# Attention trunk on one core: q, k and v of seven head pairs in product units of 512 columns over pair borders, and attention anchors set apart from the units

## The chip, the core and the metric

The kernel runs on one core of a Trainium2 chip. Its time is the device time of one execution in microseconds (us); lower is better. The names of the engines are those of the profile: PE (TensorE matmul) and PEld (its weight loads, which overlap), DVE (VectorE), ACT (ScalarE), POOL (GpSimd), SP (SyncE, which issues nearly all loads and stores). Each engine works through its own instructions in the order of the program and waits on semaphores for the others.

## What is computed

Two residual layers over 512 tokens of 1,024 features, all in float32. Layer 0 mixes tokens by attention in three dilated windows (dilations 1, 4 and 16, radius 64, 32 and 64 steps of the dilation), layer 1 by a short gated convolution; an MLP with a squared ReLU stands behind each. The change touches the attention of layer 0:

```python
def mixer_a(h, w_qkv, q_gain, k_gain, w_o, cos, sin):
    qkv = (h @ w_qkv).reshape(B, S, A_GROUPS, 3, A_HEADS, HEAD_DIM)
    for g in range(A_GROUPS):
        q = partial_rope(rms_norm(qkv[:, :, g, 0], q_gain[g]), cos, sin)
        k = partial_rope(rms_norm(qkv[:, :, g, 1], k_gain[g]), cos, sin)
        num, den, mx = dilated_group(q, k, qkv[:, :, g, 2], dil, radius)
    wts = jnp.exp(mx - jnp.max(mx, axis=0, keepdims=True))
    o = jnp.sum(wts[..., None] * num, axis=0) / jnp.sum(wts * den, axis=0)[..., None]
    return o.reshape(B, S, D_MODEL) @ w_o
```

## The kernel before, in words

**Products.** Every large product is done three times over: each float32 operand is split into a rounded part and a rest (wh and wl for weights, hgh and hgl for activations), and the three products that matter are added up in PSUM (line 128). A weight tile of 128 rows is loaded by SP into one of four buffers (wraw), rounded by ACT (wh, line 288), and the rest is taken by POOL (wl, line 289); for the first two tiles DVE does both. There are six buffers of wh and wl each.

**Units.** The q, k and v weights of one pair of heads are nine blocks of 128 columns (three dilation groups with q, k and v each). Before the change a pair has three product units of 384 columns: group A (q0, k0, q1), group B (k1, q2, k2) and group V (v of the three groups). A unit is 8 weight tiles (k) by 4 row tiles of the tokens (r), so 8 x 4 x 3 = 96 matmuls, in blocks of two weight tiles (of one in the first unit). It fills four PSUM banks (psG, one for each r). When a bank is full, it is evacuated at once: group A and B are copied to rawA and rawB by ACT (or DVE, by the bits of vA and vB), group V is scaled and split on ACT and DVE.

**The clock of the schedule.** The program is written out by a planner with a clock of its own, which has nothing to do with the chip's: a block adds (its weight tiles) x (its row tiles) x (its columns) / 2048, so a unit of 384 columns is 6 long and one of 512 columns 8. Every other step is a task with a position on that clock; between two matmuls of a unit the planner emits the tasks that are due. So the positions set the order of the instructions on every engine, and nothing else does. The whole of q, k and v is 144 long before and after.

**Attention of a pair.** Its steps hang on two anchors, tA and tB, the ends of the pair's units A and B; the scores' anchor tS equals tB. The offsets stand in PLACES (line 60: one row for pair 0, one for pairs 1 to 6, one for pair 7). The steps, with the names that are used below:
- *normalize group A* (sqA, rsA, mulA): squares on ACT, sums by reductions on DVE (stA, line 362), twelve small DVE instructions for the reciprocal square roots (lines 365 and 151 to 157), then products and the rotation on DVE (lines 371 to 378). The same for group B (stB), with three of four rotations on POOL.
- *fills* (TA, TB, line 387): four transposes on PE into a score bank (psT, three banks), rounded by ACT (q0h and so on, line 401), rest by DVE (q0l, line 403).
- *S0* (line 443) and *S12* (line 457): scores on PE, masked and reduced on DVE (lines 447 and 460), then exponentials on ACT.
- *weights of the groups* (W1 to W4), with two swaps of rows through PE (line 433).
- *N12 and N0* (lines 502 and 504): the products of the probabilities with the weights, half on DVE, half on POOL.
- *PT* (line 516): transposes of the probabilities into psT, split by ACT and DVE (pth and ptl); *PV* (line 544): their product with v; at the end the sum into oT (line 548).

The attention of a pair lies beside the units of the pairs that follow. The part of v for dilation 1 goes through DRAM and back (move_v0).

**The start.** x comes in eight column tiles. Each is transposed on PE (line 297), scaled and split into hgh and hgl by ACT (line 300) and DVE (a copy to oT, line 301, and the rest, line 302): an x fill. Eight squares of x on ACT (line 273) give the statistics of the first normalization (x_stats: lines 279 to 282 and 151 to 157, 14 DVE instructions of 4 columns). DVE also builds the rotation tables tabA and tabB (line 251) from loaded gains.

Of the kernel before, what the change touches and what calls it, by code (L numbers as in the profile page):

```python
# [35 lines left out]
def _constants():  # L36
# [10 lines left out]
    for n, b in enumerate((0, 1, 3)):  # L47
# [27 lines left out]
def trunk_kernel(ctx, tc, x, norm1, norm2, wqkv, qgain, kgain, wo, win, conv, wout, w1, w2, c_rope, c_m0, c_m12, out):
# [251 lines left out]
    def evacV(p):
        def f(r, ps):
            if r == 0:
                need("stats", 0, 1)  # L330
                st[p]["v"] = ptile(vp, [128, 4, 3, 2, 2, 64], R32, "v")
            v = st[p]["v"][:, r].rearrange("p g h s d -> p (g h) s d")
            split(v[:, :, 0], v[:, :, 1], ps[:, 0:384].rearrange("p (a d) -> p a d", d=64), rcol[:, r:r + 1])
            mark("evV", p)
            if r == 3:
                after(0.4, move_v0)

        def move_v0():

            v0 = st[p]["v0"] = ptile(vp, [128, 4, 2, 128], R32, "v0")  # L340
            sync.dma_start(v0d[p].rearrange("r c h s d -> c r (h s d)"),
                           f32(st[p]["v"])[:, :, 0].rearrange("p r h s d -> p r (h s d)"))

            def read(j, a):
                c = (32 * j + 16 + 16 * a) % 128
                sync.dma_start(f32(v0)[64 * a:64 * a + 64, j].rearrange("p h c -> p (h c)"),
                               v0d[p][:, c:c + 16].rearrange("r c h s d -> r c (h s d)"))
                mark("v0", p)
            for j in range(4):
                for a in range(2):  # L350
                    after(1.2 + 0.35 * (2 * j + a), lambda j=j, a=a: read(j, a))
        return f
# [228 lines left out]
    def mark(name, p):  # L581
        seen[name, p] = seen.get((name, p), 0) + 1

    def need(name, p, n):
        assert p < 0 or seen.get((name, p), 0) >= n, f"{name} of pair {p}: {seen.get((name, p), 0)} of {n} issued"

    def attn_tasks(p, tA, tB, c):


        tS = tB  # L590
# [9 lines left out]
        for r in range(4):  # L600
            put(tA + c["sqA"] + 0.25 * r, "sqA", lambda r=r: norm_sq(rawA, stA, 6, r, r < c["qA"]), ("evA", p, 4))
# [36 lines left out]
        for n, (h, i) in enumerate([(h, i) for h in range(2) for i in range(4)]):  # L638
            s = tS + c["P"] + c["dP"] * n + c["gP"] * (n > 3)
            put(s, "PT", lambda h=h, i=i: PT(p, h, i), ("N12" if i > 1 else "N0", p, 8))  # L640
            put(s + c["lP"], "PV", lambda h=h, i=i, n=n: PV(p, h, i, n % 4 == 0, n % 4 == 3), ("PT", p, n + 1), ("evV", p, 4),
                ("v0", p, 8))
# [374 lines left out]
```

## Time and profile before

| | |
|---|---|
| median of 3 runs (lowest, highest) | 1487.7 us (1486.6, 1487.86) |
| the profiled execution's own time | 1487.62 us |
| its span, first to last instruction | 1485.8 us |
| mean granted clock of PE | 0.997 |
| q, k, v and attention | 6.8 to 546.7 us of the span |
| output projection of the attention | 546.7 to 603.8 us |
| MLP, convolution, second MLP | 603.8 to 1485.8 us |

Times in the views count from the start of the span. A row of a timeline has start, length, engine, line, operation, output<-inputs, shapes and count, and in brackets the idle time of the engine before it and who ended it. A matmul's row names the moving operand first, then the stationary one; its length is modelled and longer than the distance to the next, so the rate is read from the starts. "st" is a bank of psT, "g" one of psG, "sm" the scores of a pair.

### The profile page before, as it was taken

The numbers are of one execution on the slowest core, as the hardware profiler recorded it, in microseconds if no ns is written. First come the engines' busy times: TensorE is split into PE (matmuls) and PEld (weight loads), VectorE is DVE, ScalarE is ACT, GpSimd is POOL, SyncE is SP. The second block draws the span as 40 slices with busy tenths as digits, with TensorE's granted clock in tenths as the row PEclk, the third lists the DMA queues.
The fourth block names the chain that finished last, engine by engine and source line by source line (L and its number), as shares of the span: only waits on it lengthen the run. The fifth ranks groups of instructions, "written<-read, shape, count | busy, mean of one in ns | idle before, by whom it ended". The sixth has DMA issues, their size and how long they took to land.

```text
span 1485.8 us, 22525 instructions
## 1 busy us (share of the span) xinstructions
PE 1474.2 (99%) x7900; PEld 1291.2 (87%) x7900; DVE 708.0 (48%) x1460; ACT 663.2 (45%) x1359; POOL 702.9 (47%) x671
## 2 busy tenths in 40 slices
PE   9899999999999999999999999999999999999998
PEld 8899999999999998888888888878888888888887
DVE  6777667676767684822021223554447330122222
ACT  5456565656556573544342332433343443333320
POOL 4444444536454444455444445444455554544442
PEclk9999999999999999999999999999999999999999
DMA  6432322323132323232222222233332222222222
GB/s 170 132 104 69 94 87 78 102 65 115 54 115 67 101 98 130 96 113 93 95 97 99 99 97 95 82 89 93 100 113 100 99 93 92 100 99 96 99 89 85
DMA packets 164509, 144.76 MB, mean 97 GB/s; under 512 B 13812, under 2 KB 125484, under 8 KB 164396
## 3 DMA queue, kind: packets, MB, share of 16 engines
q1 hardware_dynamic: 164076, 143.06, 30.7%
q8 instruction: 62, 1.02, 0.3%
q14 instruction: 51, 0.42, 0.1%
q10 hardware_dynamic: 320, 0.27, 0.1%
HBM read 134.89 MB, written 8.39 MB: 96 GB/s over the span
## 4 chain that ended last, share of the span: by engine, by line
PE 93%; DVE 3%; issue 1%; ACT 1%; DMA 1%; SPq 1%; POOL 0%; DVEq 0%; POOLq 0%; ACTq 0%
PE g L128 85%; PE o L544 3%; PE st L516 2%; PE st L457 2%; PE st L387 1%; PE st L443 1%; DMA sm<-in_x 0%; POOL wl L289 0%; DVE sm L504 0%; SPq L567 0%; ACT sqx L273 0%; PE g L873 0%; DMA wraw<-in_a_wqkv 0%; ACT wh L288 0%; PE st L433 0%
## 5 line engine op out<-in xcount | busy, mean ns | idle before, releaser
L289 POOL TENSOR_TENSOR wl<-wraw,wh 128x512 fp32r<-128x512 f32 (+1 forms) x544 | 636.9, 1192 | 702.6 <-ACT wh L288 688.3
L288 ACT CAST wh<-wraw 128x512 fp32r<-128x512 f32 (+1 forms) x544 | 300.3, 569 | 500.0 <-PE g L128 376.2
L128 PE MATMUL g<-hgBh,wl 128*128 128x512 f32 x704 | 274.3, 390 | 0.5 <-POOL wl L289 0.4
L128 PE MATMUL g<-hgBh,wh 128*128 128x512 f32 x704 | 274.0, 389 | 0.1
L128 PE MATMUL g<-hgBl,wh 128*128 128x512 f32 x704 | 273.9, 389 | 0.0
L128 PE MATMUL g<-wh,hgl 128*128 128x384 f32 x768 | 268.2, 349 | 0.3 <-DVE hgl L302 0.2
L128 PE MATMUL g<-wl,hgh 128*128 128x384 f32 x768 | 262.4, 342 | 0.0
L128 PE MATMUL g<-wh,hgh 128*128 128x384 f32 x768 | 262.0, 341 | 0.0
L805 DVE SCALAR_TENSOR_TENSOR zr<-g,R 128x512 f32<-128x512 f32 x64 | 44.0, 691 | 283.2 <-PE g L128 283.0
L128 PEld LDWEIGHTS g<-hgBh,wl 128*128 128x128 f32 x704 | 132.2, 188 | 29.6 <-POOL wl L289 2.2
L128 PEld LDWEIGHTS g<-hgBh,wh 128*128 128x128 f32 x704 | 132.2, 188 | 27.8 <-ACT wh L288 0.5
L128 PEld LDWEIGHTS g<-hgBl,wh 128*128 128x128 f32 x704 | 132.2, 188 | 27.3
L128 PEld LDWEIGHTS g<-wh,hgl 128*128 128x128 f32 x768 | 145.2, 189 | 3.3 <-DVE hgl L302 1.2
L128 PEld LDWEIGHTS g<-wh,hgh 128*128 128x128 f32 x768 | 145.5, 189 | 0.3 <-issue 0.2
L128 PEld LDWEIGHTS g<-wl,hgh 128*128 128x128 f32 x768 | 145.1, 189 | 0.4
L822 DVE TENSOR_TENSOR acc<-g,acc 128x512 f32<-128x512 f32 x32 | 22.1, 692 | 138.2 <-PE g L128 138.2
L128 PE MATMUL g<-z0h,wh 128*128 128x512 f32 x192 | 74.7, 389 | 0.0
L128 PE MATMUL g<-z0l,wh 128*128 128x512 f32 x192 | 74.7, 389 | 0.0
L128 PE MATMUL g<-z0h,wl 128*128 128x512 f32 x192 | 74.7, 389 | 0.0
L466 ACT ACTIVATE sm<-sm,mxs 128x256 f32<-128x256 f32 x128 | 63.9, 501 | 15.5 <-DVE mxs L460 12.2
L288 ACT CAST pth<-st 128x512 fp32r<-128x512 f32 x64 | 37.5, 585 | 65.4 <-PE st L516 63.0
L806 ACT ACTIVATE zz<-zr 128x512 f32<-128x512 f32 x64 | 40.5, 633 | 38.7 <-DVE zr L805 36.8
(212 smaller groups left out, 2354.4 us busy)
## 6 DMA issues: line engine op xcount, KB each, us to landing
wraw<-in_mlp_w SPq DMA_DIRECT2D x256, 256.0 KB
wraw<-in_a_wqkv SPq DMA_DIRECT2D x128, 128.0 KB
wraw<-in_a_wqkv SPq DMA_DIRECT2D x64, 192.0 KB
wraw<-in_a_wqkv SPq DMA_DIRECT2D x128, 64.0 KB
wraw<-in_b_win SPq DMA_DIRECT2D x64, 128.0 KB
v0d<-v SPq DMA_DIRECT2D x8, 512.0 KB
v<-v0d SPq DMA_DIRECT2D x64, 64.0 KB
wraw<-in_b_win SPq DMA_DIRECT2D x64, 64.0 KB
```

Of the source, the lines that this page charges most:

```text
L128: pe.matmul(unit["ps"][n][:, :width], a, b, start=st, stop=sp)
L288: act.copy(hi, src)
L289: (eng or dve).tensor_sub(lo, src, f32(hi))
L387: pe.transpose(o, raw[r][:, w, :], ident)
L443: pe.matmul(ps[h][:, 256 * b2:256 * b2 + 256], q0v(a, h, b), k0v(k, h, b), start=(q == 0), stop=(q == 2))
L457: pe.matmul(pv[:, :, g], a[:, 128 * r:128 * r + 128], k[:, 256 * r:256 * r + 256], start=(q == 0), stop=(q == 2))
L466: act.activation(t[:, h, b], t[:, h, b], AF.Exp, bias=mx(m)[:, c], scale=-1.0, accum_out=mx(d)[:, c])
L516: pe.transpose(ps[:, 128 * n:128 * n + 128], src, ident)
L544: pe.matmul(out_, stat, mov, start=first and q == 0, stop=last and q == len(ops) - 1, skip_group_check=True)
L805: dve.scalar_tensor_tensor(zr, ps, 0.0, state["R"], op0=ALU.max, op1=ALU.mult)
L806: after(0.4, lambda: act.activation(zz, zr, AF.Square))
L822: dve.tensor_add(a, ps, a)
```

## The change

Pairs 0 to 6 get 15 units of 512 columns and one of 384, in which blocks of two pairs may stand side by side; pair 7 keeps its three units of 384. The evacuation cuts a bank into runs of one pair and group, and the load merges neighbouring blocks into one transfer. v is awaited group by group. The anchors no longer follow the units: the scores' anchors are a table of eight numbers (SCORES), and tA is 6 before them; only pair 0's tA is the end of the unit that holds its group A. They stood at 12, 30, 48, 66, 84, 102, 120 and 138 before. The squares of x and the statistics move 0.7 and 0.75 later, the x fills are 1.0 apart instead of 0.75, with the blocks of the first unit.

```diff
-         dN=0.04, P=12.45, ..., xq=2.7, dxq=0.3, xs=5.35,
+         dN=0.04, P=12.45, ..., xq=3.4, dxq=0.3, xs=6.1,
+SCORES = (16.0, 34.0, 52.5, 72.0, 89.0, 106.0, 122.0, 138.0)
...
-    def evacA(p):
+    def evac_qkv(cols_):
+        runs = []
+        for i, (p, part, slot) in enumerate(cols_):
+            if runs and runs[-1][0] == (p, part) and runs[-1][2] + runs[-1][3] == slot:
+                runs[-1][3] += 1
+            else:
+                runs.append([(p, part), i, slot, 1])
         def f(r, ps):
-            need("TA", p - 1, 3)
-            (dve.tensor_copy if place(p)["vA"] >> r & 1 else act.copy)(rawA[r].rearrange("p a b -> p (a b)"), ps[:, 0:384])
-            mark("evA", p)
+            for (p, part), i, slot, n in runs:
+                src = ps[:, 128 * i:128 * (i + n)]
+                if part == "V":
+                    evac_v(p, r, slot, n, src)
+                else:
+                    raw, name, bits = (rawA, "TA", "vA") if part == "A" else (rawB, "TB", "vB")
+                    need(name, p - 1, 3)
+                    (dve.tensor_copy if place(p)[bits] >> r & 1 else act.copy)(
+                        raw[r][:, slot:slot + n].rearrange("p a b -> p (a b)"), src)
+                    for _ in range(n):
+                        mark("ev" + part, p)
         return f
...
+    def evac_v(p, r, g0, n, src):
+        if r == 0 and "v" not in st[p]:
+            need("stats", 0, 1)
+            st[p]["v"] = ptile(vp, [128, 4, 3, 2, 2, 64], R32, "v")
+        v = st[p]["v"][:, r, g0:g0 + n].rearrange("p g h s d -> p (g h) s d")
+        split(v[:, :, 0], v[:, :, 1], src.rearrange("p (a d) -> p a d", d=64), rcol[:, r:r + 1])
...
+        if r == 3 and g0 == 0:
+            after(0.4, lambda: move_v0(p))
...
-    def attn_tasks(p, tA, tB, c):
-        tS = tB
+    def attn_tasks(p, tA, tB, tS, c):
...
-            put(s + c["lP"], "PV", ..., ("PT", p, n + 1), ("evV", p, 4),
-                ("v0", p, 8))
+            put(s + c["lP"], "PV", ..., ("PT", p, n + 1),
+                (f"evV{max(i - 1, 0)}", p, 4), ("v0", p, 8))
...
-        at(0.75 * kt - 0.7 if kt else -0.95, lambda kt=kt: xT_fill(kt))
+        at(1.0 * kt - 0.7 if kt else -0.95, lambda kt=kt: xT_fill(kt))
...
-    for p in range(NPAIR):
-        add_unit(384, ld_qkv(p, (0, 0, slice(0, 2)), (2, 1, 0)), sm_stream(384), 4, ps_g, 384, evacA(p),
-                 kblocks=K1 if p == 0 else K2)
-        tA[p] = clock[0]
-        add_unit(384, ld_qkv(p, (0, 1, 1), (1, 2, slice(0, 2))), sm_stream(384), 4, ps_g, 384, evacB(p))
-        tB[p] = clock[0]
-        add_unit(384, ld_qkv(p, (0, slice(0, 3), 2)), sm_stream(384), 4, ps_g, 384, evacV(p))
-    for p in range(NPAIR):
-        attn_tasks(p, tA[p], tB[p], place(p))
+    for p in (0, 4):
+        a, b, v = ([(q, part, i) for i in range(3)] for q, part in ((p, "A"), (p, "B"), (p, "V")))
+        a1, b1, v1 = ([(q, part, i) for i in range(3)] for q, part in ((p + 1, "A"), (p + 1, "B"), (p + 1, "V")))
+        a2, b2, v2 = ([(q, part, i) for i in range(3)] for q, part in ((p + 2, "A"), (p + 2, "B"), (p + 2, "V")))
+        units += [a + b[:1], b[1:] + v[:2], v[2:] + a1, b1 + v1[:1], a2 + v1[1:2], v1[2:] + b2]
+        if p == 0:
+            a3, b3, v3 = ([(3, part, i) for i in range(3)] for part in "ABV")
+            units += [v2 + a3[2:], a3[:2] + b3[1:], b3[:1] + v3]
+        else:
+            units += [v2] + [[(7, part, i) for i in range(3)] for part in "ABV"]
+    for i, u in enumerate(units):
+        n = 128 * len(u)
+        add_unit(n, ld_qkv(u), sm_stream(n), 4, ps_g, n, evac_qkv(u), kblocks=K1 if i == 0 else K2)
+        for p, part, _ in u:
+            ends[p, part] = clock[0]
+    for p, tS in enumerate(SCORES):
+        attn_tasks(p, ends[0, "A"] if p == 0 else tS - 6.0, tS, tS, place(p))
```

The lines of the changed kernel are moved by the edit: what is line 128, 301, 302, 362, 403 and 504 before is 132, 305, 306, 374, 415 and 516 after. Three places where the order moves, all on DVE.

**DVE in the first unit.** hgl_98 and hgl_100 are the rests of x's last two column tiles, tabA and tabB the tables, "small" and "mxs" the statistics. Before:

```order
L301 COPY oT_80<-st 128x512
L302 SCALAR_TENSOR_TENSOR hgl_98<-st,cols,hgh_97 128x512
L301 COPY oT_81<-st 128x512
L302 SCALAR_TENSOR_TENSOR hgl_100<-st,cols,hgh_99 128x512
L251 TENSOR_TENSOR tabA<-rope,gb 128x8x16 x6
L251 TENSOR_TENSOR tabB<-rope,gb 128x8x16 x6
L279 TENSOR_TENSOR small<-mxs 128x4
```

And now:

```order
L255 TENSOR_TENSOR tabA<-rope,gb 128x8x16 x6
L255 TENSOR_TENSOR tabB<-rope,gb 128x8x16 x4
L305 COPY oT_80<-st 128x512
L306 SCALAR_TENSOR_TENSOR hgl_98<-st,cols,hgh_97 128x512
L255 TENSOR_TENSOR tabB<-rope,gb 128x8x16 x2
L283 TENSOR_TENSOR small<-mxs 128x4
...
L305 COPY oT_81<-st 128x512
L306 SCALAR_TENSOR_TENSOR hgl_100<-st,cols,hgh_99 128x512
```

The tables moved ahead of the last but one tile, and the statistics (13 more rows stand where the dots are) ahead of the last one.

**DVE in pair 0.** The last product of group A (rawA_111), the sums of group B (stB) and the rests of the three fills of group A. Before:

```order
L378 TENSOR_TENSOR rawA_111<-tmpR 128x6x16
L362 TENSOR_REDUCE stB<-sqq 128x6 x4
L365 SCALAR_TENSOR_TENSOR stB<-stB,small 128x24
...
L403 SCALAR_TENSOR_TENSOR q0l<-st,cols,q0h 128x512
L403 SCALAR_TENSOR_TENSOR k0l<-st,cols,k0h 128x448
L403 SCALAR_TENSOR_TENSOR k0l<-st,cols,k0h 128x64
L403 SCALAR_TENSOR_TENSOR q1l<-st,cols,q1h 128x512
```

And now:

```order
L390 TENSOR_TENSOR rawA_111<-tmpR 128x6x16
L296 SCALAR_TENSOR_TENSOR v<-g,small,v 128x4x64 x3
L415 SCALAR_TENSOR_TENSOR q0l<-st,cols,q0h 128x512
L415 SCALAR_TENSOR_TENSOR k0l<-st,cols,k0h 128x448
L415 SCALAR_TENSOR_TENSOR k0l<-st,cols,k0h 128x64
L296 SCALAR_TENSOR_TENSOR v<-g,small,v 128x4x64
L374 TENSOR_REDUCE stB<-sqq 128x6
L415 SCALAR_TENSOR_TENSOR q1l<-st,cols,q1h 128x512
L374 TENSOR_REDUCE stB<-sqq 128x6 x3
L377 SCALAR_TENSOR_TENSOR stB<-stB,small 128x24
```

Group B's reductions and square roots moved from ahead of q0l to behind it, and parts of v came in front.

**DVE at the end of pairs 5 and 6.** The products N12 (sm_131) and N0 (sm_130), the weights' copy between them, and the sums of the next pair's group A (stA). Before, as in every pair:

```order
L504 TENSOR_SCALAR sm_131<-sm_131,mxs 128x256 x4
L496 COPY mxs<-st 128x8
L504 TENSOR_SCALAR sm_130<-sm_130,mxs 128x256 x4
L289 TENSOR_TENSOR ptl<-st,pth 128x512 x2
L362 TENSOR_REDUCE stA<-sqq 128x6
```

And now, in these two pairs:

```order
L516 TENSOR_SCALAR sm_131<-sm_131,mxs 128x256 x4
L374 TENSOR_REDUCE stA<-sqq 128x6
L508 COPY mxs<-st 128x8
L516 TENSOR_SCALAR sm_130<-sm_130,mxs 128x256
L374 TENSOR_REDUCE stA<-sqq 128x6
L516 TENSOR_SCALAR sm_130<-sm_130,mxs 128x256 x3
L374 TENSOR_REDUCE stA<-sqq 128x6 x2
```

Two reductions moved in front of most of N0, and the first one ahead of the weights' copy; the small instructions of the square roots follow them, ahead of the first splits of P.

More of the change, by code (lines that the diff above doesn't have):

```diff
@@ L327, in evacV @@
[L327 to L352, printed above, removed]
+    def evac_qkv(cols_):
[5 more added lines that the diff above has]
+                runs.append([(p, part), i, slot, 1])
+        def f(r, ps):
+            for (p, part), i, slot, n in runs:
[9 more added lines that the diff above has]
+                        mark("ev" + part, p)
+        return f
@@ new lines, in evac_v @@
+    def evac_v(p, r, g0, n, src):
[4 more added lines that the diff above has]
+        split(v[:, :, 0], v[:, :, 1], src.rearrange("p (a d) -> p a d", d=64), rcol[:, r:r + 1])
+        for g in range(g0, g0 + n):
+            mark(f"evV{g}", p)
+        if r == 3 and g0 == 0:
+            after(0.4, lambda: move_v0(p))
@@ new lines, in move_v0, with read @@
+    def move_v0(p):
+        v0 = st[p]["v0"] = ptile(vp, [128, 4, 2, 128], R32, "v0")
+        sync.dma_start(v0d[p].rearrange("r c h s d -> c r (h s d)"),
+                       f32(st[p]["v"])[:, :, 0].rearrange("p r h s d -> p r (h s d)"))
+        def read(j, a):
+            c = (32 * j + 16 + 16 * a) % 128
+            sync.dma_start(f32(v0)[64 * a:64 * a + 64, j].rearrange("p h c -> p (h c)"),
+                           v0d[p][:, c:c + 16].rearrange("r c h s d -> r c (h s d)"))
+            mark("v0", p)
+        for j in range(4):
+            for a in range(2):
+                after(1.2 + 0.35 * (2 * j + a), lambda j=j, a=a: read(j, a))
@@ L600, in attn_tasks @@
         for r in range(4):
-            put(tA + c["sqA"] + 0.25 * r, "sqA", lambda r=r: norm_sq(rawA, stA, 6, r, r < c["qA"]), ("evA", p, 4))
+            put(tA + c["sqA"] + 0.25 * r, "sqA", lambda r=r: norm_sq(rawA, stA, 6, r, r < c["qA"]), ("evA", p, 12))
         put(tA + c["sqA"] + c["rsA"], "rsA", lambda: norm_rs(stA, 6), ("sqA", p, 4), ("stats", 0, 1))
@@ L608, in attn_tasks @@
         for r in range(4):
-            put(tB + c["sqB"] + 0.25 * r, "sqB", lambda r=r: norm_sq(rawB, stB, 6, r, r < c["qB"]), ("evB", p, 4))
+            put(tB + c["sqB"] + 0.25 * r, "sqB", lambda r=r: norm_sq(rawB, stB, 6, r, r < c["qB"]), ("evB", p, 12))
         put(tB + c["sqB"] + c["rsB"], "rsB", lambda: norm_rs(stB, 6), ("sqB", p, 4))
@@ L640, in attn_tasks @@
             put(s, "PT", lambda h=h, i=i: PT(p, h, i), ("N12" if i > 1 else "N0", p, 8))
[L641 to L642 removed]
+            put(s + c["lP"], "PV", lambda h=h, i=i, n=n: PV(p, h, i, n % 4 == 0, n % 4 == 3), ("PT", p, n + 1),
+                (f"evV{max(i - 1, 0)}", p, 4), ("v0", p, 8))
     K1 = tuple((k,) for k in range(KT))
@@ L663, in trunk_kernel @@
     at(c["xs"], x_stats)
-    tA, tB = {}, {}
-    for p in range(NPAIR):
-        add_unit(384, ld_qkv(p, (0, 0, slice(0, 2)), (2, 1, 0)), sm_stream(384), 4, ps_g, 384, evacA(p),
-                 kblocks=K1 if p == 0 else K2)
-        tA[p] = clock[0]
-        add_unit(384, ld_qkv(p, (0, 1, 1), (1, 2, slice(0, 2))), sm_stream(384), 4, ps_g, 384, evacB(p))
-        tB[p] = clock[0]
-        add_unit(384, ld_qkv(p, (0, slice(0, 3), 2)), sm_stream(384), 4, ps_g, 384, evacV(p))
-    for p in range(NPAIR):
-        attn_tasks(p, tA[p], tB[p], place(p))
+    units = []
+    for p in (0, 4):
[6 more added lines that the diff above has]
+            units += [v2 + a3[2:], a3[:2] + b3[1:], b3[:1] + v3]
+        else:
+            units += [v2] + [[(7, part, i) for i in range(3)] for part in "ABV"]
+    assert sorted(b for u in units for b in u) == [(p, part, i) for p in range(NPAIR) for part in "ABV" for i in range(3)]
+    ends = {}
+    for i, u in enumerate(units):
[4 more added lines that the diff above has]
+    for p, tS in enumerate(SCORES):
+        assert ends[p, "B"] <= tS and ends[p, "A"] <= tS - 6.0 or p == 0
+        attn_tasks(p, ends[0, "A"] if p == 0 else tS - 6.0, tS, tS, place(p))
     state = {}
```

27 lines of the change are left out of this document (16 added, 11 removed).

## The prediction

> **What bounds the kernel now.** I read the page first, then the busy times by stage, then the waits of the tensor engine (PE), and last the timelines at the places those name. The page's busy times:
>
> ```profile
> PE 1474.2 (99%) x7900; PEld 1291.2 (87%) x7900; DVE 708.0 (48%) x1460; ACT 663.2 (45%) x1359; POOL 702.9 (47%) x671
> ```
>
> PE is the bound, but its busy time is modelled, so the stages say more. Busy times by stage (columns: stretch, its length, then busy time and count of each engine, granted clock, DMA share, GB/s):
>
> ```profile
> 6.80:60.00 53.20, 47.94 (x280) 45.22 (x279) 42.14 (x98) 28.05 (x65) 26.12 (x31) 0.98 0.65 179
> 120.00:480.00 360.00, 360.00 (x2534) 347.50 (x2534) 255.05 (x677) 212.79 (x510) 169.12 (x204) 1.00 0.29 86
> 603.80:1485.80 882.00, 877.43 (x3879) 724.45 (x3877) 283.85 (x384) 316.14 (x541) 420.83 (x333) 1.00 0.29 96
> ```
>
> From 120 to 480 us, and again after 603.8, PE never idles. Only the first 60 us have gaps. After 603.8 nothing is touched by the change. What PE waited for up to 546 us (columns: us in total, times, longest):
>
> ```profile
> PE st L443 <- DVE q0l L403: 2.9, 1, 2.9
> PE st L297 <- DMA sm<-in_x: 1.1, 1, 1.1
> ```
>
> So a gain can come from two sources: the time of one matmul, and the waits of pair 0. Everything on DVE, ACT, POOL and the queues matters only where it makes PE wait.
>
> **The change part by part.** *Cadence.* 1,920 matmuls of 384 columns (20 units of 96) become 1,440 of 512 (15 units of 96); the order of PE has 7,364 rows before and 6,884 now, 480 fewer. Starts in stretches without attention work, first and last: 384 columns in the units (108 intervals between the two rows); 512 columns in the second MLP, where as in the units the weight tile moves (111 intervals); 512 columns in the output projection, where hgA moves (36 intervals):
>
> ```profile
> 32.01 0.34 PE L128 MATMUL g<-wl,hgh 128*128 128x384 f32 x1
> 50.73 0.34 PE L128 MATMUL g<-wl,hgh 128*128 128x384 f32 x1
> ...
> 1399.66 0.39 PE L128 MATMUL g<-wh,z0h 128*128 128x512 f32 x1
> 1424.82 0.39 PE L128 MATMUL g<-wh,z0h 128*128 128x512 f32 x1
> ...
> 554.10 0.39 PE L128 MATMUL g<-hgl,wh 128*128 128x512 f32 x1
> 562.50 0.39 PE L128 MATMUL g<-hgl,wh 128*128 128x512 f32 x1
> ```
>
> That is 18.72/108 = 173.3 ns, 25.16/111 = 226.7 ns and 8.40/36 = 233.3 ns. A line through the first two has 53.4 ns per 128 columns and 13.2 ns that do not depend on the columns. 1,920 x 173.3 = 332.7 us; 1,440 x 226.7 = 326.4 us, or 336.0 us at the slower rate. So the term lies between -6.3 and +3.3 us. Operands and roles are those of the MLP row, so I take a rate near it, 227.6 ns (a seventh of the way): **-5.0 us**.
>
> The Trainium skill ("TensorE: Matmul & The Clock Gate", section "Wait — 56ns, not 53.3ns?") gives a fixed cost of about 2.5 ns per matmul and 215.7 ns for 512 columns. By it 480 fewer matmuls would be worth an estimated 1.2 us, not 6.3. The rows above disagree: 226.7 and 173.3 ns both stand 13 ns over the columns' share, and the measurement decides.
>
> *Pair 0's waits.* The anchors move apart: pair 0's scores now start 8 units of clock after its group A (16 against 8) instead of 6 (12 against 6). PE around the waits, then DVE at the same time:
>
> ```profile
> 50.90 0.49 PE L387 MATMUL st<-ident,rawA 128*128 128x128 f32 x3
> 52.15 0.33 PE L387 MATMUL st<-ident,rawA 128*128 128x128 f32 x1 [0.76 <-DVE rawA L378]
> ...
> 55.81 0.34 PE L128 MATMUL g<-wh,hgl 128*128 128x384 f32 x1
> 59.05 0.55 PE L443 MATMUL st<-k0h,q0h 64*128 64x256 f32 x1 [2.90 <-DVE q0l L403]
> ...
> 65.06 0.34 PE L128 MATMUL g<-wh,hgl 128*128 128x384 f32 x1
> ...
> 66.03 0.39 PE L443 MATMUL st<-k0h,q0h 64*128 64x256 f32 x2
> 66.94 0.44 PE L128 MATMUL g<-wl,hgh 128*128 128x384 f32 x1
> ```
>
> ```profile
> 52.01 2.15 DVE L362 TENSOR_REDUCE stB<-sqq 128x6 f32<-128x384 f32 x4
> 54.20 0.91 DVE L365 SCALAR_TENSOR_TENSOR stB<-stB,small 128x24 f32<-128x24 f32 x1
> 58.16 0.74 DVE L403 SCALAR_TENSOR_TENSOR q0l<-st,cols,q0h 128x512 fp32r<-128x512 f32 x1
> 60.26 1.95 DVE L371 TENSOR_TENSOR rawB<-rawB,stB 128x384 f32<-128x384 f32 x4
> 63.18 0.41 DVE L447 CUSTOM_DVE_ANT_0 sm<-st,msk 128x256 f32<-128x256 f32 x1
> ```
>
> ```profile
> 58.21:65.04 6.83, 5.76 (x23) 5.30 (x24) 6.35 (x19) 1.81 (x5) 3.92 (x6) 0.50 0.00 0
> ```
>
> q0l waited behind group B's reductions and square roots (52.01 to 58.16), S0 waited for q0l, and the granted clock fell to 0.50 for 6.83 us. The price: from 55.81 to 65.06 PE did one matmul, one S0 (0.91 us when undisturbed, 66.03 to 66.94, plus some 0.27 before it) and ten matmuls with a longer first one (0.1): 9.25 us against 0.91 + 0.27 + 10 x 0.173 + 0.28 = 3.2. That is 6.05 us, and 0.92 more at the fourth rawA transpose (52.15 where 51.23 was due). Now q0l stands ahead of B's reductions, S0 comes 2.5 clock units (6.8 us at 12 x 226.7 ns a unit) behind the last fill instead of 0.5, and the statistics that kept DVE busy after group A are done earlier. **-7.0 us**; I see nothing that would keep more than 2 us of it.
>
> *What is late next: the second S0.* Its score bank is freed by the masks of the first S0, and these stand on DVE behind group B's normalization. After unit 1 ends, ACT's evacuation, two casts and the first square take some 2.1 us (estimate), then by the DVE rows above the reductions with q1l 2.15 + 0.65, the square roots 54.20 to 58.16 = 4.0, the products 60.26 to 63.18 = 2.9, two masks 0.7: 12.5 us. PE reaches the second S0 after 3.6 units x 2.72 + a fill 0.44 + an S0 0.91 = 11.1 us. **+1.4 us**, between 0 and 3.
>
> *The first unit.* Tables and statistics now stand on DVE ahead of the splits of x's last two tiles:
>
> ```profile
> 26.73 0.74 DVE L302 SCALAR_TENSOR_TENSOR hgl<-st,cols,hgh 128x512 fp32r<-128x512 f32 x1
> 27.39 1.96 DVE L251 TENSOR_TENSOR tabA<-rope,gb 128x128 f32<-128x128 f32 x6
> 29.28 1.29 DVE L251 TENSOR_TENSOR tabB<-rope,gb 128x128 f32<-128x128 f32 x6
> 30.49 0.15 DVE L279 TENSOR_TENSOR small<-mxs 128x4 f32<-128x4 f32 x1
> 35.88 0.16 DVE L157 SCALAR_TENSOR_TENSOR small<-mxs,small 128x4 f32<-128x4 f32 x1
> 30.54 3.92 POOL L289 TENSOR_TENSOR wl<-wraw,wh 128x384 fp32r<-128x384 f32 x4 [2.34 <-ACT wh L288]
> ```
>
> The 14 statistics took 5.5 us (30.49 to 36.04), six of them 4.0 us while POOL ran, the rest 0.19 each; all at 0.19 would be 2.7, so I take 3.9 with POOL busy part of the time. From a fill's emission to the matmul that needs its split there are 0.7 blocks of 3.2 us (12 x 226.7 ns and a fill) and two matmuls: 2.65 us. For the last tile DVE has two tables 0.4, statistics 3.9, copy 0.6 and split 0.7 to do: 5.6, less about 0.9 by which the block before it is late itself, 2.1 late (1 to 4). For the tile before: ten tables 2.8 and 1.3 of its own on a queue that is about level, 0.7 late. Against that goes the wait for x (1.1): a block is 0.64 us longer, and its fill comes three matmuls later. **+1.7 us**, between -1.5 and +5.
>
> *Pairs 5 and 6.* Their successors start 16 clock units after them instead of 18. So on DVE one reduction of the next pair's group A stands before the copy of the weights and one behind the first of the products N0; before, all four came after the products. N0 on DVE, and PE at the transposes that read it, for a pair of before:
>
> ```profile
> L362 DVE TENSOR_REDUCE stA<-sqq 128x6 f32<-128x384 f32 x32 | 16.8, 548 | 12.0 <-ACT sqq L361 11.1
> 360.63 1.82 DVE L504 TENSOR_SCALAR sm<-sm,mxs 128x256 f32<-128x256 f32 x4
> 361.34 0.74 PE L516 MATMUL st<-ident,sm 128*128 128x128 f32 x4
> 361.84 0.42 PE L128 MATMUL g<-wl,hgh 128*128 128x384 f32 x1
> ```
>
> The second product ends near 361.6, and PE's four transposes there take 0.50 us (361.34 to 361.84) where 0.35 is usual: they come with no slack. Two reductions are 1.1 us later, twice: 2.2, of which I take **+1.8 us**, between 0 and 6, since the crowding of the shorter distance has no row of its own.
>
> *At nothing:* DVE gets 48 instructions more, ACT 29 (evacuations cut at group borders), SP 32 loads more (352 against 320, its bytes unchanged). In the row of 120 to 480 us DVE is busy 71%, ACT 59%, POOL 47%, DMA 29%: the cover is there, and each split or evacuation has over 4 us until a matmul asks for it (18 matmuls of 226.7 ns). The 40 casts and 40 subtractions saved on ACT and POOL lie under the same cover. If it fails, PE waits at a unit's border, 19 borders of some 0.3 us (a short copy): up to 6 us, as much as the upper bound of the term above.
>
> The sum against the profiled execution's own 1,487.6 us (span 1,485.8 and 1.8 around it; the median of the runs, 1,487.7, is the same within 0.1): -5.0 - 7.0 + 1.4 + 1.7 + 1.8 = -7.1, so **1,480.5 us**.
>
> **The rivals.** *Everything is hidden.* The three new waits don't come and the cadence is the MLP's: -6.3 - 7.0 = -13.3, 1,474.3 us. For it: PE never idled between 120 and 480 us with DVE 71% busy. Against it: the order of DVE in the first unit, where work is put ahead of a split that PE needs within 2.65 us.
>
> *The units run at the slow rate.* The 233.3 ns were measured in the stage right behind, with hgA as an operand and attention work around. Then the cadence costs 3.3 instead of saving 5.0: 1,488.8 us, no change. Against it: in the units the excess over the columns' share is that of the fast rows, 13 ns, at 384 columns.
>
> *The first unit's wait halves the clock.* If the last tile's split is 4 us late instead of 2.1, PE idles longer than the 2.90 us in front of S0, and the granted clock falls to 0.50 for 6.83 us as in the row above, which costs half of that, 3.4: 1.9 + 3.4 more, 1,485.8 us. The Trainium skill (same page, section "What's actually happening") has free-running windows of about 3.4 us and half the clock after one idle window; the row's 6.83 us are two of them, so the trace agrees.
>
> *Slower: DVE falls behind in the closer pairs.* The place is pairs 3 to 6, whose successors start 17 or 16 units after them: the next pair's square roots and products come to stand among the transposes of P, whose three score banks DVE has to free. DVE works 255.05/360 of the time, 47 us of the some 67 us of a pair (the stage's 546.7 - 6.8 over 8); at 16 units, 2 x 2.72 = 5.4 us less, 77% of it. The price of one long wait is known, 6.05 us with its half clock. It decides at about 10 us in all: two such waits instead of the 1.8 give 1,490.8, four 1,503. For it: the order of DVE has the square roots before the first two splits of P. Against it: at 71% no wait at all was seen.
>
> That the change does not do what it says can be left out: the order has the 480 rows fewer.
>
> **How the numbers follow.** Chances: the forecast 0.46, all hidden 0.20, the slow rate 0.12, the halved clock 0.12, DVE behind 0.10. The time is that of the likeliest, 1,480.5. From 1,473 to 1,489 the range takes in all but the last case and a part of the second, with the bounds of the single terms (the forecast alone: 1,476 to 1,485). A measurement of this kernel tells 0.2%, 3.0 us, from no change: faster is below 1,484.7, slower above 1,490.7. Faster: nearly all of the first two and a third of the halved clock, 0.68. Same: most of the slow rate and of the halved clock, 0.20. Slower: 0.12.
>
> **What would show it.** Cadence: starts of matmuls of 512 columns in the units, 227 to 228 ns; 233 would show the first term wrong. Pair 0: no wait of PE for q0l or the fourth rawA transpose, and no granted clock of 0.50 near 60 us. First unit: a wait of PE for hgl of the last tile, some 2 us, with the statistics just before it on DVE. Second S0 of pair 0: a wait for a mask of the first. Pairs 5 and 6: a wait of about 1 us at the first transposes of P. The prediction is wrong if waits of PE between 100 and 540 us add up to more than 5 us, or if the clock falls anywhere behind the first unit.

## The result, and the profile after

The changed kernel takes 1510.64 us (median of 4 runs, 1506.9 to 1512.58) against 1487.78 us (4 runs, 1486.6 to 1488.16): ratio 1.0152, 95% interval 1.0139 to 1.0166. It is slower by 22.9 us where 7 us less had been forecast. The profiled execution is the shortest, 1506.9 us with a span of 1505.1 us and a mean granted clock of 0.999; the other three show 0.994 to 0.996, so they have more of the halved stretches described below (the profile of experiment 1, whose waits are the same within 0.1 us, has three of them and 0.996).

The page and the busy times by stage of the changed kernel, in the columns of the views of before:

```profile
PE 1479.2 (98%) x7420; PEld 1224.7 (81%) x7420; DVE 714.0 (47%) x1488; ACT 659.6 (44%) x1355; POOL 697.5 (46%) x631
```

```profile
6.80:60.00 53.20, 50.22 (x225) 38.36 (x224) 34.74 (x81) 26.69 (x60) 28.18 (x27) 1.00 0.69 188
120.00:480.00 360.00, 347.61 (x2051) 283.28 (x2050) 249.06 (x661) 198.57 (x476) 153.49 (x162) 1.00 0.27 80
566.20:623.10 56.90, 56.73 (x321) 46.73 (x321) 33.94 (x69) 29.14 (x62) 25.45 (x26) 1.00 0.44 140
623.10:1505.10 882.00, 877.46 (x3879) 724.40 (x3877) 284.10 (x384) 315.37 (x541) 421.03 (x333) 1.00 0.30 96
364.80:368.20 3.40, 3.40 (x13) 2.81 (x12) 2.25 (x3) 2.30 (x5) 1.32 (x2) 0.50 0.39 113
```

The output projection (546.7 to 603.8 us before, 566.2 to 623.1 now) and all behind it last as long as they did. The whole loss stands in front of it: that stage ends 19.5 us later. Between 120 and 480 us PE was never idle before; now it idles 12.4 us there, with DVE busy 69% of the time, less than the 71% of before. What PE waits for between 60 and 570 us (before, between 66 and 546 us, no group reached 0.2 us):

```profile
PE st L455 <- DVE mxs L459: 3.3, 2, 2.8
PE o L556 <- DVE v L296: 2.5, 3, 2.0
PE st L399 <- POOL rawB L390: 2.2, 4, 1.0
PE g L132 <- ACT rawA L334: 1.9, 2, 1.1
PE st L528 <- DVE sm L516: 1.8, 3, 0.9
PE st L445 <- DVE k1l L415: 1.5, 1, 1.5
PE st L399 <- DVE ptl L293: 1.5, 1, 1.5
PE o L556 <- DVE ptl L293: 1.1, 2, 0.6
PE st L528 <- DVE ptl L293: 0.6, 1, 0.6
PE st L469 <- DVE k2l L415: 0.2, 1, 0.2
```

That is 16.6 us in ten groups, none of them large. All end on DVE, or on a step of POOL or ACT that had itself waited for DVE (one row of each):

```profile
217.72 0.27 ACT L334 COPY rawA<-g 128x128 f32<-128x128 f32 x1 [3.38 <-DVE v L296]
...
359.80 0.85 POOL L388 TENSOR_TENSOR tmpRP<-rawB,tabB 128x192 f32<-128x192 f32 x1 [4.16 <-DVE rawB L383]
```

One more price hangs on them: behind the waits of 362 and 363 us the granted clock is 0.50 for 3.4 us (the last row of the stages above). In the 3.41 us ahead of that, PE had been busy for 1.72 us.

The second change is the rate. PE in the stretch of units without attention work, first and last of 100 intervals, with the wait in front of it:

```profile
34.95 0.50 PE L132 MATMUL g<-wh,hgl 128*128 128x512 f32 x1 [1.71 <-DVE hgl L306]
35.28 0.40 PE L132 MATMUL g<-wh,hgh 128*128 128x512 f32 x1
...
58.71 0.39 PE L132 MATMUL g<-wl,hgh 128*128 128x512 f32 x1
```

23.43/100 = 234.3 ns, not 227.6. At these rates the 1,440 matmuls take 337.4 us where 1,920 of 173.3 ns took 332.7: 480 fewer instructions cost 4.7 us more.

How one wait comes about is seen in pair 0, DVE first and PE behind it:

```profile
66.65 0.18 DVE L377 SCALAR_TENSOR_TENSOR stB<-stB,small 128x24 f32<-128x24 f32 x1
66.87 0.18 DVE L155 TENSOR_SCALAR stB<-stB 128x24 int32<-128x24 int32 x1
67.08 1.30 DVE L156 TENSOR_SCALAR stB<-stB 128x24 int32<-128x24 int32 x1
68.41 1.22 DVE L159 TENSOR_TENSOR stB<-stB 128x24 f32<-128x24 f32 x1
...
71.40 2.56 DVE L383 TENSOR_TENSOR rawB<-rawB,stB 128x384 f32<-128x384 f32 x4
...
74.97 0.42 DVE L459 CUSTOM_DVE_ANT_0 sm<-st,msk 128x256 f32<-128x256 f32 x1
```

```profile
72.67 0.38 PE L455 MATMUL st<-k0h,q0h 64*128 64x256 f32 x1
75.81 0.38 PE L455 MATMUL st<-k0h,q0h 64*128 64x256 f32 x1 [2.76 <-DVE mxs L459]
```

The masks of the first S0, whose scores PE had written by 69.7 us, stand in DVE's order behind group B's square roots and products. PE reaches the second S0 at 72.67 us, DVE the masks at 74.97. PE waits 2.76 us while DVE works without a pause.

### The profile page after: what moved, and what is told of

It reads as the page before. It is cut to its first block, busy times and chain, and to the rows that moved or that the text cites. A ratio compares the mean times of both kernels' runs of the same rounds, so it can differ in the third digit from the quotient of the medians.

```text
span 1505.1 us, 21552 instructions
## 1 busy us (share of the span) xinstructions
PE 1479.2 (98%) x7420; PEld 1224.7 (81%) x7420; DVE 714.0 (47%) x1488; ACT 659.6 (44%) x1355; POOL 697.5 (46%) x631
## 4 chain that ended last, share of the span: by engine, by line
PE 82%; DVE 8%; issue 4%; ACT 2%; POOL 2%; DMA 1%; SPq 1%; POOLq 0%; DVEq 0%; ACTq 0%
PE g L132 75%; PE o L556 2%; PE st L469 1%; DVE sm L516 1%; PE st L528 1%; PE st L399 1%; DMA wraw<-in_a_wqkv 1%; POOL wl L293 1%; DVE stA L374 1%; PE st L455 1%; ACT wh L292 1%; DVE ptl L293 1%; POOL tmpRP L388 1%; SPq L593 0%; DVE tmpR L388 0%
## 5 line engine op out<-in xcount | busy, mean ns | idle before, releaser
L292 ACT CAST wh<-wraw 128x512 fp32r<-128x512 f32 (+1 forms) x504 | 291.3, 597 | 483.7 <-PE g L132 393.7
L132 PE MATMUL g<-wh,hgh 128*128 128x512 f32 (+1 forms) x608 | 238.4, 392 | 1.9 <-ACT rawA L334 1.9
L132 PE MATMUL g<-wh,hgl 128*128 128x512 f32 (+1 forms) x608 | 237.8, 391 | 2.3 <-DVE hgl L306 2.1
L132 PE MATMUL g<-wl,hgh 128*128 128x512 f32 (+1 forms) x608 | 239.5, 394 | 0.1
L132 PEld LDWEIGHTS g<-wh,hgl 128*128 128x128 f32 x608 | 115.2, 189 | 22.3 <-DVE hgl L306 5.0
L132 PEld LDWEIGHTS g<-wh,hgh 128*128 128x128 f32 x608 | 115.0, 189 | 20.5 <-ACT rawA L334 2.7
L132 PEld LDWEIGHTS g<-wl,hgh 128*128 128x128 f32 x608 | 114.9, 189 | 17.3 <-POOL wl L293 0.5
```

The costliest lines, as they stand in the source:

```text
L132: pe.matmul(unit["ps"][n][:, :width], a, b, start=st, stop=sp)
L292: act.copy(hi, src)
```

## The experiments

Three causes were in question: the rate of the 512-column matmuls, the anchors (too close to each other, or in the wrong place), and the units over pair borders (v and the evacuations in pieces). The ratios are to the kernel before, with 95% intervals.

**1 and 2. 32 and 64 bytes of padding.** hgA, which the units and the output projection read at 512 columns, starts at address 180192 (bytes within a partition of the on-chip memory, by the program's allocation), 32 bytes past a multiple of 64; hgB and z of the MLP start at multiples of 64. The second run has 16 in place of 8.

```diff
+    ptile(open_pool("pad", side="right", bufs=1), [128, 8], F32, "pad")
     oTp = open_pool("oT", side="right", bufs=1)
```

> The changed kernel with 32 bytes of padding that shift oT and hgA, so that hgA starts at a multiple of 64 bytes instead of 32 bytes past one; nothing else. Theory 'address' (512-column matmuls that read hgA pay some 7 ns because hgA lies 32 bytes off): the starts in the units go from 234 ns to 227 and in the output projection from 233 to 227, 1440 x 7.3 + 1.6 = 12 us off, 1498 to 1500 us, or a few us less of a gain if the waits of PE grow in turn. Rival 'interruption' (the attention's insertions put PE in a slower pattern): 234 ns as before, 1510 us.

> Control: the changed kernel with 64 bytes of padding, which move hgA as well but leave it 32 bytes past a multiple of 64. Theory 'address': no change, 1507 to 1513 us, 234 ns. A rival in which any move of hgA to another place is enough would give the 1498 us of the 32-byte padding.

1510.65 us (1.0159, 1.0142 to 1.0176) and 1510.99 us (1.0159, 1.0138 to 1.0179). With 32 bytes, 100 intervals of the units:

```profile
35.79 0.39 PE L132 MATMUL g<-wh,hgh 128*128 128x512 f32 x1
...
59.11 0.39 PE L132 MATMUL g<-wl,hgh 128*128 128x512 f32 x1
```

233.2 ns: a multiple of 64 is not what matters. The theory in this form falls.

**3. The same 32 bytes in the kernel before.**

> The kernel before with the same 32 bytes of padding. Theory 'address, seen only at 512 columns': the 1920 matmuls of 384 columns stay at 173.3 ns, the output projection goes from 233.3 to 226.7 ns, 240 x 6.6 = 1.6 us off, 1486.1 us. If 384 columns paid too, 1920 x 7 = 13 us would go, 1474 us. Theory 'interruption': 1487.7 us.

1489.57 us (1.0013, 1.0004 to 1.0022), 2 us slower and expected by neither. 46 intervals of the units:

```profile
149.54 0.34 PE L128 MATMUL g<-wh,hgl 128*128 128x384 f32 x1
...
157.68 0.34 PE L128 MATMUL g<-wh,hgh 128*128 128x384 f32 x1
```

8.14/46 = 177.0 ns instead of 173.3 here; the other stretches of 40 and more intervals stand between 174.6 and 176.8. The address of hgA does touch the rate, only not as thought. Over all units, without the first distance behind an insertion, the mean is 175.6 ns instead of 174.0, 3 us for 1,920 matmuls; in the output projection it is 230.0 instead of 233.4, 0.7 us less for 192. That accounts for the 2 us.

**4. The anchors alone.** The kernel before, its 24 units and its start, with the anchors of the change:

```diff
+SCORES = (16.0, 34.0, 52.5, 72.0, 89.0, 106.0, 122.0, 138.0)
...
-        attn_tasks(p, tA[p], tB[p], place(p))
+        attn_tasks(p, tA[p] if p == 0 else SCORES[p] - 6.0, SCORES[p], place(p))
```

> The kernel before, with its 24 units of 384 columns and its start, but with the anchors of the changed kernel (16, 34, 52.5, 72, 89, 106, 122, 138; group A 6 earlier, for pair 0 at the end of its unit). Theory 'the closer anchors make the waits': pair 0's 7.0 us go, the waits of the changed kernel come back as there (second S0 of pair 0, pairs 3 to 6), some 8 to 12 us, 1489 to 1493 us. Rival 'the units over pair borders make them' (v and the evacuations in pieces): no wait over 0.5 us after 60 us, 1480 to 1482 us.

1516.62 us (1.0199, 1.0184 to 1.0214): slower than the whole change, beyond both expectations. Its largest group of waits, and two of the seven, DVE and then PE:

```profile
PE g L131 <- DVE v L295: 13.3, 7, 2.7
```

```profile
137.22 0.18 DVE L368 SCALAR_TENSOR_TENSOR stB<-stB,small 128x24 f32<-128x24 f32 x1
...
141.12 0.55 DVE L374 TENSOR_TENSOR rawB<-rawB,stB 128x384 f32<-128x384 f32 x1
141.59 0.61 DVE L295 SCALAR_TENSOR_TENSOR v<-g,small,v 128x384 fp32r<-128x384 f32 x1
142.12 2.17 DVE L374 TENSOR_TENSOR rawB<-rawB,stB 128x384 f32<-128x384 f32 x3
...
145.23 1.13 DVE L295 SCALAR_TENSOR_TENSOR v<-g,small,v 128x384 fp32r<-128x384 f32 x2
```

```profile
142.26 0.44 PE L131 MATMUL g<-wh,hgh 128*128 128x384 f32 x1 [1.97 <-DVE v L295]
...
145.89 0.69 PE L131 MATMUL g<-wh,hgh 128*128 128x384 f32 x1 [2.33 <-DVE v L295]
```

The next unit needs the bank of psG that holds v, and v's split stands on DVE behind the square roots, masks and products of group B. With the anchors of before, group V ended when none of that was queued. Six of the seven waits come in pairs 1, 2 and 5, where group V ends 2, 1.5 and 2 clock units behind the scores' anchor, and the seventh (0.5 us) in pair 0, where it ends 2 behind. None comes in pairs 3, 4, 6 and 7, where it ends 0, 1, 4 and 6 behind; before, it ended 6 behind in every pair. Pairs 1 and 2 have distances of 18 and 18.5, as wide as before. So it is not closeness that makes these waits but where the anchors stand against the ends of the units, and units over pair borders are not needed for it. That they add waits of their own is seen in the changed kernel only (pair 1's PV for the last piece of v, 2.0 us). Half clock adds to the time: 17.1 us of it stand in this profile, against 3.4 in the change's.

**5. The sides of memory swapped.** hgA goes to 50816, hgB from there to 174048:

```diff
-    hgp = open_pool("hgA", side="right", bufs=1)
+    hgp = open_pool("hgA", bufs=1)
...
-    ab = open_pool("attn", bufs=1)
+    ab = open_pool("attn", side="right", bufs=1)
```

The pools of v and of the MLP's trunk change to the right side in the same way.

> The changed kernel with tiles moved in memory only: hgA (read by the units and the output projection) goes to the low addresses, from 50816, where the MLP's hgB lay; the attention's tiles and hgB go to the high side (hgB from 174048). Theory 'place' (a matmul of 512 columns is slower when it reads a tile at those high addresses): the units and the output projection go from 234 to 227 ns, and the MLP's matmuls that read hgB from 227 to 233 ns, so some 12 us less up to the MLP and 2100 x 6.6 = 14 us more in it. Theory 'stage' (the attention's insertions, or what else runs in the units): 234 ns in the units and 227 in the MLP as before, 1510 us.

1519.36 us (1.0213, 1.0194 to 1.0233). First and last of 100 intervals in the units, and of 87 in the first MLP:

```profile
35.40 0.40 PE L132 MATMUL g<-wh,hgh 128*128 128x512 f32 x1
...
58.07 0.39 PE L132 MATMUL g<-wl,hgh 128*128 128x512 f32 x1
...
639.91 0.40 PE L132 MATMUL g<-hgBh,wh 128*128 128x512 f32 x1
...
660.22 0.40 PE L132 MATMUL g<-hgBh,wh 128*128 128x512 f32 x1
```

226.7 ns in the units and 233.4 ns in the MLP: the slow rate has moved with the address, from hgA to hgB. Theory "stage" falls. But 50816 is also a multiple of 128, and 174048 lies 96 past one, so "place" and "alignment" are not told apart yet. The time up to the MLP shrank by 1.2 us only (it starts at 621.9 us, in the change at 623.1): the waits behind 60 us are 18.5 us instead of 16.6, and two stretches of 3.4 us at half clock stand there instead of one.

**6. A shorter DVE.** One step of the square root's iteration instead of three, so the normalization is left unfinished:

```diff
-        for _ in range(3):
+        for _ in range(1):
```

> The changed kernel with one step of the reciprocal square root's iteration instead of three (part of the normalization is left out): 6 small DVE instructions fewer in each of 16 normalizations of a group and in the statistics, some 1.1 to 3 us of DVE time each. Theory 'DVE's queue': the waits of PE behind DVE (second S0 of pairs 0 and 3, the transposes, group B of pair 4) shorten, from 16.8 us after 60 us to 9 to 12, and with fewer halved clocks 1500 to 1505 us. Rival 'the steps stand too close on PE, whatever DVE does' : 1508 to 1511 us, the same waits within 2 us.

1493.06 us (1.0034, 1.0019 to 1.0049), 17.6 us faster than the change. DVE's busy time over the whole span:

```profile
PE 1475.5 (99%) x7420; PEld 1224.9 (82%) x7420; DVE 679.3 (46%) x1368; ACT 660.3 (44%) x1355; POOL 696.9 (47%) x631
```

34.7 us less of DVE, 120 instructions fewer, on an engine that is busy less than half of the span, take 17.6 us from the time. Between the two profiled executions it is 14.0 us: the waits behind 60 us are 7.9 us instead of 16.6 (pair 1's wait for v is gone), the first unit's wait for the last split is 0.5 instead of 1.7, and some 4 us are not assigned. The medians differ by more than the profiles, as the change's other executions had the lower clocks named above (here all have 0.999 or 1.0). Theory "DVE's queue" holds, and more strongly than expected: the time lies below its range.

**7. Pair 0's step alone.** The kernel before, with nothing changed but five offsets of pair 0 (TA of the fills, S0 of the scores, E0 of their exponentials, X and lX of the row swap):

```diff
-TA=7.6, ..., S0=2.6, dS=1.0, E0=3.75, X=5.5, lX=2.0
+TA=7.9, ..., S0=5.0, dS=1.0, E0=6.15, X=7.7, lX=0.8
```

> The kernel before, in which only pair 0's scores and fills move: fills 0.3 later (TA 7.9), the scores and their exponentials 2.4 later (S0 5.0, E0 6.15), and the row swap kept where it was (X 7.7, lX 0.8). The prediction's term of pair 0: its wait for q0l and the halved clock go, -6 to -7 us, 1480.5 to 1482 us. Rival 'the wait only moves on' (to the second S0, or to the row swap behind it): within 2 us of 1487.4.

1482.07 us (0.9964, 0.9951 to 0.9977), 5.3 us faster than before; the best of all. What PE waits for in it after 60 us, and its stages:

```profile
PE st L457 <- DVE k2l L403: 1.0, 1, 1.0
PE g L128 <- DVE oT L739: 0.2, 1, 0.2
```

```profile
120.00:480.00 360.00, 360.00 (x2521) 347.96 (x2520) 254.70 (x678) 210.98 (x509) 169.13 (x204) 1.00 0.30 87
```

The 2.90 us in front of S0 and the halved clock are gone; 1.0 us comes back later at S12.

**8. Other anchors for the changed kernel.** The units stay; BEHIND is how far each pair's tA stands ahead of its scores' anchor (6 in the change; the first entry isn't used):

```diff
-SCORES = (16.0, 34.0, 52.5, 72.0, 89.0, 106.0, 122.0, 138.0)
+SCORES = (16.0, 35.5, 51.5, 72.5, 89.0, 106.0, 122.0, 138.0)
+BEHIND = (6.0, 7.0, 5.25, 8.0, 6.0, 5.75, 5.5, 5.75)
...
-TA=7.6, ..., S0=2.6, dS=1.0, E0=3.75
+TA=7.2, ..., S0=2.0, dS=1.6, E0=3.15
...
```

> The changed kernel with its units as they are and other anchors: scores at 16, 35.5, 51.5, 72.5, 89, 106, 122, 138, group A 7, 5.25, 8, 6, 5.75, 5.5, 5.75 ahead of them for pairs 1 to 7, and pair 0's fills and scores 0.4 to 0.6 earlier with 1.6 between its two S0. Theory 'the anchors' place against the units' ends and against the neighbour pairs makes the waits': waits after 60 us fall from 16.8 to 4 to 8 us, no halved clock behind 60 us, 1493 to 1499 us. Rival 'the closer pairs are too much for DVE at any place of the anchors' or 'the units in pieces make them': over 13 us of waits stay, 1505 us or more. By both the cadence stays at 234 ns, so it stays slower than the kernel before.

1493.08 us (1.0038, 1.0025 to 1.0052), 17.6 us faster than the change (14.5 between the profiled executions, 11.4 of it waits) by moves of 1.5 clock units at most. From pair 3 on the distances are 16.5, 17, 16 and 16, no wider than the change's 17, 17, 16 and 16. What is left behind 60 us sums to 5.2 us, with one wait over 1 us:

```profile
PE g L133 <- DVE rawB L335: 1.9, 1, 1.9
```

So neither the short distances nor the pieces cost much as such. What costs is which instructions stand ahead of which on DVE.

**9. 96 bytes of padding.** hgA at 180096, a multiple of 128, still at the high addresses.

```diff
+    ptile(open_pool("pad", side="right", bufs=1), [128, 24], F32, "pad")
```

> The changed kernel with 96 bytes of padding, which move hgA by 96 bytes to a multiple of 128 (180096); it stays at the high addresses. Theory 'alignment to 128 bytes' (all tiles that were read at 227 ns lie at multiples of 128: hgB and z in the changed kernel, hgA with the sides swapped; all at 233 ns lie 32, 64 or 96 past one): 227 ns in the units and the output projection, 10 + 1.6 us off, 1498 to 1500 us. Rival 'place' (the high addresses themselves): 233 to 234 ns, 1508 to 1512 us.

1506.7 us (1.0130, 1.0116 to 1.0144). 94 intervals in the units, and then the first six behind a piece of attention and the end of that stretch (34 intervals from 163.32):

```profile
38.42 0.39 PE L132 MATMUL g<-wh,hgh 128*128 128x512 f32 x1
...
59.75 0.39 PE L132 MATMUL g<-wl,hgh 128*128 128x512 f32 x1
...
163.32 0.40 PE L132 MATMUL g<-wh,hgh 128*128 128x512 f32 x1
...
164.72 0.39 PE L132 MATMUL g<-wh,hgh 128*128 128x512 f32 x1
...
171.07 0.39 PE L132 MATMUL g<-wl,hgh 128*128 128x512 f32 x1
```

226.9 ns: alignment it is, and "place" falls. But the time falls by 4 us, not by 11. Behind each insertion the first matmuls come at 233 ns (1.40/6) and the stretch of 34 averages 227.9. Over all the units, without the first distance behind an insertion, the mean is 229.3 ns against 233.9 in the change, some 6 us instead of 10. Of these the waits take back 1.9 us: 18.5 us instead of 16.6 after 60 us. How much half clock an execution meets differs too (mean clocks of 0.995 to 0.998 in the four here, 0.994 to 0.999 in the change), so the rest is not divided further.

**10. All three together.** Anchors of 8, padding of 9, and the statistics and tables behind the last x fill (xs 7.45, tb 7.5).

> The changed kernel with the other anchors of the run before, hgA at a multiple of 128 bytes, and the statistics and tables behind the last x fill (xs 7.45, tb 7.5). Theory 'the three causes add': 1493.1 less 11.6 for the cadence, less 1.9 and half of 3.4 for the first unit's wait and its halved clock, 1477 to 1480 us, faster than the kernel before and than pair 0's step alone. Rivals: with 'place' for the cadence 1488 to 1491 us; if the faster units make PE wait for DVE again, 1482 to 1486 us.

1486.48 us (0.9995, 0.9986 to 1.0004): no measurable difference from the kernel before. The three causes don't add, and the time lies half a microsecond above the range of the rival in which the faster units make PE wait again. The first unit's wait for the last split is gone, as expected; the cadence gave some 229 ns and not 227, and 6.2 us of waits after 60 us stayed, 5.2 in experiment 8.

**11. Experiments 7 and 9 together, on the kernel before.**

> The kernel before with pair 0's scores and fills later (as in the run with that step alone, 1482.1 us) and with hgA at a multiple of 128 bytes. Theory 'alignment': the output projection at 227 ns, 1.6 us off, the units of 384 columns at 173.3 ns as they were, 1480.5 us. Rival 'place': 1482 us.

1482.34 us (0.9966, 0.9954 to 0.9979), as experiment 7. The output projection lasts 56.7 instead of 57.0 us; of the 1.6 us expected (6.6 ns for each of the 192 matmuls that the trace has there would be 1.3) only 0.3 came. Its matmuls too stand behind insertions and average 229.2 ns, not 227; in its longest stretch, 36 intervals, they come at 227.8.

**12. The largest waits of 10 taken on.** Anchors moved by up to 0.3, other row tiles evacuated by DVE (bits for pairs 1, 3, 5 and 7), the second half of P's transposes 0.2 earlier, the products of group B 0.1 earlier.

> The tuned and aligned kernel of the run before (1486.5 us, some 7 us of waits and one halved clock left) with its largest waits taken on: anchors moved by up to 0.5, pair 1 to 6's group B products 0.1 earlier, the second half of the transposes of P 0.2 earlier, and other row tiles evacuated by DVE (none of rawB's last two for pairs 1, 3 and 5). Theory 'only waits stand between the long units and the short ones': 2 to 4 us of waits after 60 us and no halved clock, 1481 to 1483 us, level with pair 0's step alone (1482.1). Rival 'DVE is too full, each move makes another wait': 1486 us or more.

1488.76 us (1.0007, 0.9998 to 1.0016). The rival holds, for these moves at least: the 1.9 us at rawB are gone, and others stand in their place, 9.0 us after 60 us instead of 6.2:

```profile
PE o L559 <- DVE oT L563: 4.5, 3, 2.4
PE o L559 <- DVE ptl L296: 2.3, 3, 1.6
```

## Why the prediction was wrong, step by step

*Cadence, -5.0.* Wrong in sign: +4.7. The step that failed is "Operands and roles are those of the MLP row, so I take a rate near it". The operands are alike in form but not in address, and the output projection, which reads the same hgA, was the row to go by; the rival with its 233.3 ns had only 0.12. Its objection, that 384 columns show no excess, says nothing: at 384 columns an hgA in that place costs nothing (table below).

*Pair 0's waits, -7.0.* Right as a mechanism: in the change PE waits neither for q0l nor for rawA there, and with that step alone the kernel gains 5.3 us, with 1.0 us given back at S12.

*The second S0, +1.4 (0 to 3).* Right in place and cause, 2.8 us. Of the 1.4 us more, 0.7 are the square roots (66.65 to 71.36 us, 4.7 instead of 4.0, two small instructions taking 2.5 us while POOL ran) and 0.7 the products and the rotation (71.40 to 74.97 us, 3.6 instead of 2.9).

*The first unit, +1.7.* Right in place and cause, too high in sum: 1.71 us at the last tile's split where 2.1 were forecast, none at the tile before (0.7), and the 1.1 us for x are gone, so +0.6. Moving the statistics and the tables behind the last fill removed the wait (experiment 10). Not forecast were 0.6 us for a load of small parameters at 31.64 us.

*The rival "The first unit's wait halves the clock".* In the change's profile it doesn't. In those of experiments 2, 8 and 9 it does, for 3.4 us, although the wait is no longer there, 1.5 to 1.6 us. So a wait longer than 2.90 us isn't needed. Nor had PE been idle for a whole 3.41 us before: ahead of the fall at 58.21 us in the kernel before it had been busy 1.35 us of the last 3.41. Only the lengths, 6.83 and 3.41 us, agree with the reading in the prediction.

*Pairs 5 and 6, +1.8.* The size is right by luck: the three waits for N0 sum to 1.8 us, but only 0.9 us of it lies behind 480 us; the longest, 0.9, is in pair 3, which the term left out.

*"At nothing".* This is the step that failed most. "DVE is busy 71% ... the cover is there" took an average for a distance. The 71% say that DVE has time in a pair, not that a given split comes before the matmul that needs it. DVE works in order; a chain of twelve small instructions and four products stands for 7 us ahead of whatever the planner put behind it. Which evacuation, mask or split that is depends on the anchors' place against the ends of the units, and the change moved that place in every pair. Some 12 us of waits come from here, and the halved clock with them. Both signs that the prediction had named for this came: the waits between 100 and 540 us add up to 13.7 us, and the clock fell behind the first unit. (The count was off too, without weight in this: the pages have 28 more instructions on DVE, 1,488 against 1,460, and 4 fewer on ACT.) "Each split or evacuation has over 4 us" counted from the end of its own matmuls to the next use, without the instructions that stand ahead of it.

*The rival "DVE falls behind in the closer pairs"* named the engine and the sign, but took the distance for the cause, with 0.10. More than half of the waits, 9.3 us, lie before 230 us, in pairs 0 to 2, and experiment 8 removes two thirds of all without widening the distances behind pair 3.

*The sum*, for the profiled executions: -6.3 for pair 0 (experiment 7's 5.3 and the 1.0 that it gave back), +4.7 cadence, +1.7 - 1.1 first unit, +0.6 for the load, +16.6 waits behind 60 us, +1.7 for 3.4 us at half clock: 17.9 of the 19.3 us. 1.4 us are not assigned. The medians differ by 3.6 us more, with the lower clocks of the other three executions.

## What to carry to other kernels

Between a producer and its consumer, count the instructions that stand in between on the producer's engine, in the program's order; a busy share says nothing about them. When a step is tied to another one's end (here an anchor to a unit), look for what was tuned by that tie before cutting it, and try the part of a change that has its own reason alone first: pair 0's five numbers are worth 5.3 us, the whole change loses 22.9. A rate is taken from rows that read the same tile, not only the same shape.

## What the runs showed of the hardware that was not expected

- **Alignment of a matmul's operand.** Mean distance of starts in ns, in stretches without interruption (of 27 to 100 matmuls with hgA stationary, of 36 with hgA moving, of 46 at 384 columns), by how far hgA starts past a multiple of 128 bytes; the weights' tiles lie at multiples of 128 in all of them:

| bytes past | 512 columns, hgA stationary | 512 columns, hgA moving | 384 columns, hgA stationary |
|---|---|---|---|
| 0 (experiments 5, 9, 11) | 226.8 to 228.4 | 227.4 to 227.9 | 173.3 to 173.4 |
| 32 (experiment 2) | 233.0 to 233.3 | 233.4 | 173.6 |
| 64 (experiments 1 and 3) | 233.2 to 233.5 | 229.2 | 174.6 to 177.0 |
| 96 (before and the change) | 233.9 to 234.4 | 233.3 | 173.3 to 173.4 |

  hgB as the moving tile shows the same ends: 226.7 at 0 in the kernel before, 233.4 at 96 (experiment 5). The Trainium skill ("SBUF — State Buffer", section "Operand start alignment") asks only for a multiple of the element size and says that its runs timed nothing; the runs here agree that it is legal and show a price. Why the price depends so on the column count is open.
- **A slow start behind an insertion.** With aligned tiles the first matmuls of 512 columns behind a piece of attention come at some 233 ns (the rows of experiment 9) and settle to 226.7 only after about eight. In units that are interrupted every few microseconds the long matmul seldom reaches its own rate: of the 170 stretches in experiment 9, 35 hold more than eight distances. With hgA 96 past (the change) no such settling is seen.
- **Small DVE instructions beside POOL.** POOL's two subtractions wl in the changed kernel, at the time of the DVE rows shown above:

```profile
67.04 2.54 POOL L293 TENSOR_TENSOR wl<-wraw,wh 128x512 fp32r<-128x512 f32 x2 [1.71 <-ACT wh L292]
```

DVE's instructions of 24 columns take 0.18 us each, and two of them 1.30 and 1.22 us inside these 2.54. The Trainium skill ("Trainium Architecture — The Big Picture", section "What this means for kernel authors") calls the port shared by DVE and GpSimd an exclusive lock; the row agrees. Not every DVE instruction is held, though: beside POOL's pair before (62.78 to 65.34 us) a reduction and q1l took their usual 0.55 and 0.75 us.
- **Half clock, and when it comes.** Apart from the start and the end of the span, every stretch at half clock in these traces lasts 3.41 or 6.83 us, and within one trace they start whole multiples of 3.41 us apart: in experiment 2 at 35.25, 76.21, 192.26 and 369.76 us, 12, 34 and 52 times 3.413. Where these steps lie against the kernel's start differs from one execution to the next. So the same wait can halve the clock in one and not in another: behind the second S0's wait of some 2.8 us the clock falls in experiments 1, 2 and 9 (77.12, 76.21 and 75.92 us), but not in the change's profile and not in experiment 5. Which share of busy time in a step decides was not measured.
